# Six of layer 1's eleven pairs of up projections by Strassen's seven products, in three passes

## Chip, core and metric

One core of a Trainium2 chip runs the whole program. The metric is the device time of one execution in microseconds (us). The engines are TensorE (PE; its weight loads are listed apart as PEld), VectorE (DVE), ScalarE (ACT), GpSimd (POOL) and the DMA queue of SyncE (SP).

## What is computed

A trunk of two layers on 512 tokens of width 1024: layer 0 is a convolution module and a SwiGLU feed-forward part, layer 1 is windowed attention and a second SwiGLU part, then a last norm. The change is in the SwiGLU part of layer 1 alone:

```python
def swiglu_ffn(x, w_up, w_down):
    gate, up = jnp.split(x @ w_up, 2, axis=-1)
    return (jax.nn.silu(gate) * up) @ w_down

h = h + swiglu_ffn(rmsnorm(h, norm_ffn[l]), ffn_w_up[l], ffn_w_down[l])
```

`w_up` is 1024 x 5632 (gate and up, 2816 columns each), `w_down` is 2816 x 1024. All values are float32.

## The kernel before

**Layout.** Activations are kept transposed: a tile has 128 channels as partitions and the 512 tokens as columns. `h[0..7]` are the eight tiles of the residual. The norm's gain is applied to `h` before the projection (`split_scaled`, L431 and L432) and the factor 1/rms of each token after it.

**Three passes.** A float32 product is made from numbers cut into a high and a low part. `mm3` (L273 to L279) issues three matmuls for each 128x128 block of weights: high weights by high rows (L277), high weights by low rows (L278), low weights by high rows (L279), each with its own weight load. Here 512 columns of rows stream through each.

**Chunks.** Weights come as chunks of 128x1024 floats in the order of `PLAN`. `load` (L200) issues a chunk's DMA on SP into one of four `raw` buffers. `advance` cuts a chunk: ACT casts the high part (`whi`, L216), DVE subtracts it from the raw chunk (`wlo`, L219). It runs three chunks ahead of the one in use; `whi` and `wlo` have four buffers each, so a chunk is cut when PE is done with the chunk four places before it.

**Up projections.** The 2816 columns are eleven pairs of 128-column tiles. A pair has four chunks: contraction half 0 and 1, each for gate and for up (in the code `half` and `which`), and 96 matmuls. `ffn_up` ends a pair with the evacuation: DVE multiplies the four banks by 1/rms (L558, L560), ACT applies silu (L559), POOL multiplies gate by up (L561), and ACT and DVE cut the result into the hidden tile (L435, L436).

**Down projections.** After some pairs a part's down chunks follow (48 matmuls for each pair), and DVE adds the banks to `h` (L519). Before, layer 1 has the parts of pairs 0 to 5, 6 to 8, and the last two pairs 9 and 10, whose down projection is the block-wise end of the program (L1203, L1213).

**Around the first pair.** The output projection of attention ends in `h`. For each tile of `h`, `on_h` makes the cut and scaled rows (ACT L431, DVE L432) and a square (ACT L384) that is added up on POOL (L388). The sum over channels is a matmul (L398), then `ms` (DVE L400), the power -1/2 on POOL (L402), a diagonal (DVE L405), a matmul that spreads it (L424), and the copy `rsbc` (L418), which the evacuations need.

**Order.** The code gives the order in which work is issued; a scheduler at build time then orders the instructions of each engine by a timeline of its own, so an engine's queue can differ from the code. On the chip each queue runs strictly in order.

## Time and profile before

| | |
|---|---|
| three timed runs | median 1083.57 us (1082.81 to 1086.43) |
| the profiled execution | 1083.34 us, of which the span from first to last instruction is 1081.5 us |
| granted TensorE clock in it, mean | 0.999 of full speed |
| first sum over channels of layer 1's feed-forward part (L398) | at 722.20 us |
| start of its pair 1 (the spread of 1/rms stands just ahead) | 734.50 us |
| start of the block-wise end | 1050.43 us |
| HBM read, written | 118.20 MB, 5.24 MB |

A row of a group or of a timeline names the line of the kernel, the engine, the operation and the tiles (out <- in). In a group the mean of one is in ns; a timeline begins with the start and the length in us. Ends of matmuls are modelled, so PE's pace is read from the starts.

### The profile page before, as it was taken

The numbers are of one execution on the slowest core, as the hardware profiler recorded it, in microseconds if no ns is written. First come the engines' busy times: TensorE is split into PE (matmuls) and PEld (weight loads), VectorE is DVE, ScalarE is ACT, GpSimd is POOL, SyncE is SP. The second block draws the span as 40 slices with busy tenths as digits, with TensorE's granted clock in tenths as the row PEclk, the third lists the DMA queues.
The fourth block names the chain that finished last, engine by engine and source line by source line (L and its number), as shares of the span: only waits on it lengthen the run. The fifth ranks groups of instructions, "written<-read, shape, count | busy, mean of one in ns | idle before, by whom it ended". The sixth has DMA issues, their size and how long they took to land.

```text
span 1081.5 us, 14727 instructions
## 1 busy us (share of the span) xinstructions
PE 1074.3 (99%) x5506; PEld 913.0 (84%) x5506; DVE 633.6 (59%) x1034; ACT 490.0 (45%) x883; POOL 330.6 (31%) x430
## 2 busy tenths in 40 slices
PE   9999999999999999999999999999999999999997
PEld 8888889999988888888888777788888888888886
DVE  3999988977777545443555656564544333444353
ACT  3887887755565333232352655443323211322233
POOL 3999997710222111111120434141111100110010
PEclk9999999999999999999999999999999999999999
DMA  9238045565555422322222212222222222222202
GB/s 356 81 102 95 10 147 198 182 226 195 176 178 192 156 98 85 111 97 97 97 81 98 73 45 79 78 98 98 90 106 98 97 97 97 95 96 95 96 30 78
DMA packets 39555, 124.39 MB, mean 115 GB/s; under 512 B 4251, under 2 KB 10556, under 8 KB 39484
## 3 DMA queue, kind: packets, MB, share of 16 engines
q1 hardware_dynamic: 38764, 122.36, 33.7%
q10 hardware_dynamic: 720, 1.10, 0.3%
q8 instruction: 43, 0.70, 0.3%
q14 instruction: 28, 0.23, 0.1%
HBM read 118.20 MB, written 5.24 MB: 114 GB/s over the span
## 4 chain that ended last, share of the span: by engine, by line
PE 98%; issue 1%; DMA 1%; POOL 0%; ACT 0%; SPq 0%; POOLq 0%; DVE 0%
PE bank L277 23%; PE bank L278 23%; PE bank L279 23%; PE bank L674 10%; PE bank L309 5%; PE bank L275 4%; PE bank L310 3%; PE bank L1213 2%; PE bank L1071 1%; PE bank L1113 1%; PE bank L1100 1%; PE bank L772 1%; DMA both<-in_lead_dram 1%; PE bank L662 1%; PE bank L424 0%
## 5 line engine op out<-in xcount | busy, mean ns | idle before, releaser
L277 PE MATMUL bank<-quad,whi 128*128 128x512 f32 (+1 forms) x1200 | 439.2, 367 | 0.0
L279 PE MATMUL bank<-quad,wlo 128*128 128x512 f32 (+1 forms) x1200 | 439.0, 366 | 0.0
L278 PE MATMUL bank<-quad,whi 128*128 128x512 f32 (+1 forms) x1200 | 438.6, 365 | 0.0
L219 DVE TENSOR_TENSOR wlo<-raw,whi 128x1024 fp32r<-128x1024 f32 x186 | 258.0, 1388 | 303.2 <-ACT whi L216 298.7
L216 ACT CAST whi<-raw 128x1024 fp32r<-128x1024 f32 x186 | 195.3, 1050 | 358.2 <-PE bank L278 305.9
L277 PEld LDWEIGHTS bank<-quad,whi 128*128 128x128 f32 x1200 | 226.4, 189 | 37.7 <-issue 1.6
L279 PEld LDWEIGHTS bank<-quad,wlo 128*128 128x128 f32 x1200 | 226.4, 189 | 36.9 <-issue 0.6
L278 PEld LDWEIGHTS bank<-quad,whi 128*128 128x128 f32 x1200 | 226.4, 189 | 35.8 <-issue 0.2
L561 POOL TENSOR_TENSOR tmp<-tmp,tmp 128x512 f32<-128x512 f32 x34 | 48.1, 1416 | 408.8 <-DVE tmp L560 393.5
L716 POOL TENSOR_TENSOR pr<-pr,pr 128x256 f32<-128x256 f32 x208 | 156.5, 794 | 7.8 <-ACT pr L715 7.7
L723 DVE SCALAR_TENSOR_TENSOR bank<-apad,wdw,bank 128x256 f32<-128x256 f32 x248 | 112.6, 486 | 3.4
L715 ACT ACTIVATE pr<-apad,wdw 128x256 f32<-128x256 f32 x208 | 98.2, 501 | 14.7 <-POOL pr L716 12.7
L674 PE MATMUL bank<-quad,w 128*128 128x256 f32 x448 | 98.7, 380 | 0.0
L674 PEld LDWEIGHTS bank<-quad,w 128*128 128x128 f32 x448 | 84.9, 190 | 11.8 <-DVE bank L723 0.2
L388 POOL TENSOR_TENSOR tmp<-tmp,tmp 128x256 f32<-128x256 f32 (+1 forms) x35 | 38.6, 1103 | 149.1 <-ACT tmp L384 112.1
L309 PE MATMUL bank<-quad,whi 128*128 128x512 f32 x212 | 75.9, 398 | 0.0
L559 ACT ACTIVATE tmp<-tmp 128x512 f32<-128x512 f32 x34 | 21.4, 632 | 93.0 <-DVE tmp L558 93.0
L310 PE MATMUL bank<-quad,wlo 128*128 128x256 f32 x212 | 59.3, 280 | 0.0
L1090 POOL TENSOR_SCALAR sc<-sc,sm 128x256 f32<-128x256 f32 (+1 forms) x64 | 31.2, 507 | 52.9 <-DVE sm L1088 52.6
L309 PEld LDWEIGHTS bank<-quad,whi 128*128 128x128 f32 x212 | 39.7, 188 | 8.4
L560 DVE TENSOR_TENSOR tmp<-bank,rsbc 128x512 f32<-128x512 f32 x34 | 23.5, 691 | 32.4 <-PE bank L279 32.4
L310 PEld LDWEIGHTS bank<-quad,wlo 128*128 128x128 f32 x212 | 40.0, 189 | 1.3
(167 smaller groups left out, 921.2 us busy)
## 6 DMA issues: line engine op xcount, KB each, us to landing
raw<-in_W_dram SPq DMA_DIRECT2D x198, 512.0 KB, 3.5
w<-in_W_dram SPq DMA_DIRECT2D x14, 512.0 KB, 8.6
fd<-fs SPq DMA_DIRECT2D x1, 3072.0 KB, 34.0
h<-in_xT_dram SPq DMA_DIRECT2D x8, 256.0 KB, 8.6
bias<-fd SPq DMA_DIRECT2D x8, 256.0 KB, 4.5
both<-in_lead_dram SPq DMA_DIRECT2D x3, 512.0 KB, 6.3
out_dram<-hg SPq DMA_DIRECT2D x4, 256.0 KB, 2.0
out_dram<-hg ACTq DMA_DIRECT2D x4, 256.0 KB, 2.3
```

Of the source, the lines that this page charges most:

```text
L216: on_act = nc.scalar.copy(hi, r).ins
L219: latest[:] = [on_act, lo_engine[0].tensor_sub(lo, r, f32(hi)).ins]
L277: nc.tensor.matmul(out, w[0], x[0], start=start, stop=False)
L278: nc.tensor.matmul(out, w[0], x[1], start=False, stop=False)
L279: nc.tensor.matmul(out, w[1], x[0], start=False, stop=stop)
L309: nc.tensor.matmul(first[2], first[0], first[1], start=start, stop=False)
L310: nc.tensor.matmul(second[2], second[0], second[1], start=False, stop=stop)
L561: nc.gpsimd.tensor_mul(t2, t1, t2)
L674: mm = nc.tensor.matmul(self.pb[:, w * W2:(w + 1) * W2], w1_of(ct, w, k), x[k] if x else xg[k][:, tok], start=k == 0, stop=k == KT - 1)
L715: on_act = nc.scalar.mul(pr, a[:, j:j + W2], tap(j))
L716: on_pool = nc.gpsimd.tensor_add(pr, acc, pr)
L723: on_dve = nc.vector.scalar_tensor_tensor(yt if i == nd - 1 else c, src, tap(i), c if i else self.shift, op0=ALU.mult, op1=ALU.add)
```

## The change

Pairs 1, 3, 5, 6, 8 and 9 are made by Strassen's method in Winograd's form. The weights of a pair are a 2x2 block matrix: A11, A12, A21, A22, where the first index is the 128-column tile and the second the contraction half, each for gate and up side by side. The rows are B11 to B22, where the first index is the contraction half and the second the token half. Seven products take the place of eight. Each product is one chunk of 24 matmuls of 256 columns; a pair has 168. Pairs 0, 2, 4, 7 and 10 stay as before.

- Sums of weights, on POOL, each as two instructions of 128x512 (gate, up): S1 = A21 + A22, S2 = S1 - A11, S3 = A11 - A21, S4 = A12 - S2. They stand in the new pool `seven` (four buffers). A sum is cut by one cast and one subtraction as a chunk was; a plain block A11, A12 or A22 by two of each, of half the size.
- Sums of rows (`Rows.sums`): beside pair 0, ACT makes float32 copies of the eight scaled tiles (L724), POOL makes T1, T3, T2 and T4 from them (L731, 128x1024 each), and ACT and DVE cut each.
- Combination: each product is one bank. ACT copies the first and S1's product out, DVE adds the other five to the float32 tile `up` (L792 to L801, S2's product needs two), POOL adds twice (L794, L795). DVE multiplies by 1/rms in two instructions of 128x1024 (L805), then silu, product and cut as before.
- Raw chunks: the four chunks of such a pair stay in the four `raw` buffers till their last block is cut or summed.
- Parts: 0 to 2, 3 to 5, 6 to 8, then 9 and 10.
- The squares of the eight tiles are added up on DVE (L461) and not on POOL, and the sum over channels is issued after the first chunk of pair 0, not after the second.
- The DMA of the last norm's gain is the last load on SP, since its pool is now opened after pair 10.

```diff
-HALVES1 = ((0, 6), (6, 9))
+HALVES1 = ((0, 3), (3, 6), (6, 9))
+SEVEN = ("A11 B11", "S3 T3", "S1 T1", "S2 T2", "A12 B21", "S4 B22", "A22 T4")
+SEVENS = (1, 3, 5, 6, 8, 9)
+SEVEN_FIRST = ("A11 B11", "S1 T1", "S3 T3", "S2 T2", "A12 B21", "S4 B22", "A22 T4")
...
+            if name == "S1":
+                nc.gpsimd.tensor_add(s[name], a["A21"], a["A22"])
+            elif name == "S2":
+                nc.gpsimd.tensor_sub(s[name], s["S1"], a["A11"])
+            elif name == "S3":
+                nc.gpsimd.tensor_sub(s[name], a["A11"], a["A21"])
+            else:
+                nc.gpsimd.tensor_sub(s[name], a["A12"], s["S2"])
...
-        load(u + DMA_AHEAD)
-        while stream["split"] < min(len(PLAN), u + SPLIT_AHEAD):
+        load(SLOTS[min(len(SLOTS) - 1, u + SPLIT_AHEAD - 1)][0] + 1 + DMA_AHEAD - SPLIT_AHEAD)
+        while stream["split"] < min(len(SLOTS), u + SPLIT_AHEAD):
...
+            src = seven_sources(*blocks)
+            if len(src) == 1:
+                split_weights(hi, lo, src[0])
+                continue
+            for e in range(2):
+                split_weights(*(w[:, e * 512:(e + 1) * 512].rearrange("p (k c) -> p k c", k=4) for w in (hi, lo)), src[e])
...
+        def on_h(self, i):
+            split_scaled(self.x[i], h[i], col(self.gain, i))
+            self.rms.add(h[i])
+        def sums(self):
+            f = [quad(F32) for _ in range(2)]
+            for i in range(KT):
+                nc.scalar.mul(f[i // 4][:, i % 4, :], h[i], col(self.gain, i))
+            b11, b12, b21, b22 = (x[:, :, s] for x in f for s in HALF)
...
+            for name, t, f, a, b in (("T1", t1, nc.gpsimd.tensor_sub, b12, b11), ("T3", b12, nc.gpsimd.tensor_sub, b22, b12),
+                                     ("T2", b11, nc.gpsimd.tensor_add, b12, b11), ("T4", b21, nc.gpsimd.tensor_sub, b21, b11)):
+                f(t, a, b)
+                yield
+                both = quads.tile([P, 2, 4, 256], F32R, tag="quad", name=uid("rows"))
+                self.block[name] = [both[:, a] for a in range(2)]
+                split(self.block[name], t)
...
+            for n, name in enumerate(order_of(layer, pair)):
+                w = get_seven(layer, pair, n)
+                a, b = name.split()
+                x = rows.block[b]
+                r = acc[a] = bank().rearrange("p (a s) -> p a s", a=2)
+                for which in range(2):
+                    for k in range(4):
+                        mm3(r[:, which], [v[:, which, k, :] for v in w], [x[e][:, k, :] for e in range(2)],
+                            which == 0 and k == 0, which == 1 and k == 3)
+                if a == "A11":
+                    nc.scalar.copy(c11, r)
+                elif a == "S1":
+                    nc.scalar.copy(c22, r)
+                elif a == "S2":
+                    nc.vector.tensor_add(c12, r, c11)
+                    nc.vector.tensor_add(c21, acc["S3"], c12)
+                    nc.gpsimd.tensor_add(c12, c12, c22)
+                    nc.gpsimd.tensor_add(c22, c21, c22)
+                elif a == "A12":
+                    nc.vector.tensor_add(c11, r, c11)
+                elif a == "S4":
+                    nc.vector.tensor_add(c12, r, c12)
+                elif a == "A22":
+                    nc.vector.tensor_add(c21, r, c21)
...
+                nc.vector.tensor_mul(c[:, m], c[:, m], rs_bc)
+                gate = c[:, m, :, 0, :]
+                nc.scalar.activation(gate, gate, AF.Silu)
+                t = temp()
+                nc.gpsimd.tensor_mul(t.rearrange("p (s q) -> p s q", s=2), gate, c[:, m, :, 1, :])
+                split(hid[2 * (pair - lo) + m], t)
```

**What moves in the queues.** First PE, from the end of pair 0's first chunk to the start of its second, before the change. `quad1121` and `quad1122` are the high and low rows of contraction half 0, banks 1150 to 1153 the pair's four banks:

```order
L278 MATMUL bank1151_6658<-quad1122_6536,whi1135_6568 128x512
L279 MATMUL bank1151_6658<-quad1121_6535,wlo1136_6569 128x512
L277 MATMUL bank1152_6659<-quad1121_6535,whi1138_6598 128x512
L278 MATMUL bank1152_6659<-quad1122_6536,whi1138_6598 128x512
L279 MATMUL bank1152_6659<-quad1121_6535,wlo1139_6599 128x512
L277 MATMUL bank1153_6660<-quad1121_6535,whi1138_6598 128x512
```

The same place of PE with the change. `quad1112` and `quad1113` are the rows of contraction half 0, `quad1114` and `quad1115` those of half 1:

```order
L351 MATMUL bank1145_6655<-quad1113_6476,whi1135_6572 128x512
L352 MATMUL bank1145_6655<-quad1112_6475,wlo1136_6573 128x512
L350 MATMUL bank1144_6654<-quad1114_6477,whi1149_6660 128x512
L351 MATMUL bank1144_6654<-quad1115_6478,whi1149_6660 128x512
L352 MATMUL bank1144_6654<-quad1114_6477,wlo1150_6661 128x512
L350 MATMUL bank1144_6654<-quad1114_6477,whi1149_6660 128x512
```

Before, the second chunk still reads half 0; now it reads half 1, and the up part of half 0 (`whi1138`) comes third, behind the sum over channels.

POOL around pair 0, before: the last of the sums of squares, 1/rms, and the evacuations of pairs 0 and 1:

```order
L388 TENSOR_TENSOR tmp1142_6641<-tmp1141_6635,tmp1142_6641 128x512
L388 TENSOR_TENSOR tmp1143_6647<-tmp1142_6641,tmp1143_6647 128x512
L402 TENSOR_TENSOR rs1162_6728<-ms1161_6726,mhalf_141 128x4
L561 TENSOR_TENSOR tmp1172_6796<-tmp1171_6795,tmp1172_6796 128x512
L561 TENSOR_TENSOR tmp1174_6804<-tmp1173_6803,tmp1174_6804 128x512
```

With the change (L731 is T1, T3, T2, T4 in turn; L255, L259, L257, L261 are S1, S3, S2, S4):

```order
L731 TENSOR_TENSOR t11160_6739<-quad1158_6729 128x1024
L255 TENSOR_TENSOR sum1171_6789<-raw1137_6600,raw1155_6699 128x512
L259 TENSOR_TENSOR sum1183_6848<-raw1137_6600 128x512
L259 TENSOR_TENSOR sum1183_6848<-raw1148_6658 128x512
L257 TENSOR_TENSOR sum1187_6881<-sum1171_6789,raw1137_6600 128x512
L731 TENSOR_TENSOR quad1158_6729<-quad1159_6730,quad1158_6729 128x4x256
L255 TENSOR_TENSOR sum1171_6789<-raw1148_6658,raw1161_6741 128x512
L261 TENSOR_TENSOR sum1194_6945<-raw1155_6699,sum1187_6881 128x512
L475 TENSOR_TENSOR rs1153_6695<-ms1152_6693,mhalf_141 128x4
L731 TENSOR_TENSOR quad1158_6729<-quad1158_6729 128x4x256
L257 TENSOR_TENSOR sum1187_6881<-sum1171_6789,raw1148_6658 128x512
L731 TENSOR_TENSOR quad1159_6730<-quad1159_6730,quad1158_6729 128x4x256
```

Eight sums of weights and four of rows stand between the first of them and the evacuation of pair 0, and 1/rms (L475) stands among them.

POOL at the end of pair 5, before (the evacuations of pairs 4, 5 and 6, two instructions each):

```order
L561 TENSOR_TENSOR tmp1252_7356<-tmp1251_7355,tmp1252_7356 128x512
L561 TENSOR_TENSOR tmp1254_7364<-tmp1253_7363,tmp1254_7364 128x512
L561 TENSOR_TENSOR tmp1272_7496<-tmp1271_7495,tmp1272_7496 128x512
L561 TENSOR_TENSOR tmp1274_7504<-tmp1273_7503,tmp1274_7504 128x512
L561 TENSOR_TENSOR tmp1340_8016<-tmp1339_8015,tmp1340_8016 128x512
L561 TENSOR_TENSOR tmp1342_8024<-tmp1341_8023,tmp1342_8024 128x512
```

With the change (`raw1351` and `raw1354` are the first two chunks of pair 6; L809 is pair 5's product of gate and up):

```order
L795 TENSOR_TENSOR up1314_7827<-up1314_7827 128x512
L809 TENSOR_TENSOR tmp1342_8060<-up1314_7827 128x512
L259 TENSOR_TENSOR sum1372_8242<-raw1351_8104 128x512
L809 TENSOR_TENSOR tmp1343_8066<-up1314_7827 128x512
L259 TENSOR_TENSOR sum1372_8242<-raw1354_8134 128x512
```

A sum of pair 6 (L259, S3) now stands ahead of the second half of pair 5's evacuation. The same is found at the end of pair 8 with pair 9's S3.

More of the change, by code (lines that the diff above doesn't have):

```diff
@@ L49, with by_seven, order_of, ups @@
 NPARAM = _c
+SEVEN = ("A11 B11", "S3 T3", "S1 T1", "S2 T2", "A12 B21", "S4 B22", "A22 T4")
+SEVENS = (1, 3, 5, 6, 8, 9)
+SEVEN_FIRST = ("A11 B11", "S1 T1", "S3 T3", "S2 T2", "A12 B21", "S4 B22", "A22 T4")
+def by_seven(layer, pair):
+    return layer == 1 and pair in SEVENS
+def order_of(layer, pair):
+    return SEVEN_FIRST if pair == SEVENS[0] else SEVEN
+def ups(layer, pair):
+    return [("up", layer, pair, half, which) for half in range(2) for which in range(2)]
+def slot_plan(plan):
+    slots = []
+    for i, c in enumerate(plan):
+        if c[0] != "up" or not by_seven(c[1], c[2]):
+            slots.append((i, None))
+        elif c[3:] == (0, 0):
+            slots += [(i + (3 if n else 1), (c[1], c[2], n)) for n in range(7)]
+    return slots
 def chunk_plan():
@@ L61, in ffn @@
         for pair in range(lo, hi):
-            for half in range(2):
-                for which in range(2):
-                    plan.append(("up", layer, pair, half, which))
+            plan.extend(ups(layer, pair))
         for g in range(2):
@@ L82, in chunk_plan @@
                 plan.append(("o", part * 2 + kp, g))
-    ffn(1, *HALVES1[0])
-    ffn(1, *HALVES1[1])
+    for part in HALVES1:
+        ffn(1, *part)
     for pair in range(*LAST):
-        for half in range(2):
-            for which in range(2):
-                plan.append(("up", 1, pair, half, which))
+        plan.extend(ups(1, pair))
     for kp in range(*LAST):
@@ L95 @@
 PLAN = chunk_plan()
+SLOTS = slot_plan(PLAN)
+AT = {c: i for i, c in enumerate(PLAN)}
 NATIVE = {i for i in range(PLAN.index(("up", 0, 1, 0, 0)))}
@@ L477, in ffn_part @@
         lo, hi = (HALVES0, HALVES1)[layer][part]
-        hid = ffn_up(layer, lo, hi, xg, tok, rms, twin, plain)
+        hid = ffn_up7(layer, lo, hi, xg, pool7) if layer else ffn_up(layer, lo, hi, xg, tok, rms, twin, plain)
         w = tok.stop - tok.start
@@ new lines, in plain_pair @@
+    def plain_pair(layer, pair, rows, hid, i):
+        banks = accs(512)
+        steps = None
+        for half in range(2):
+            for which in range(2):
+                w = get("up", layer, pair, half, which)
+                order = [(k, m) for k in range(4) for m in range(2)]
+                if half == 1:
+                    order = [(k, m) for m in range(2) for k in range(4)]
+                for k, m in order:
+                    mm3(banks[which * 2 + m], [a[:, k, m * P:(m + 1) * P] for a in w], rows.x[half * 4 + k],
+                        half == 0 and k == 0, half == 1 and k == 3)
+                if half == 0 and which == 0:
+                    rows.rms.step1()
+                    continue
+                if pair == 0:
+                    steps = steps or rows.sums()
+                    for _ in range(1 + half):
+                        next(steps, None)
+        rs_bc = rows.rms.step2()
+        hid.grow()
+        for m in range(2):
+            t1, t2 = temp(), temp()
+            nc.vector.tensor_mul(t1, banks[m], rs_bc)
+            nc.scalar.activation(t1, t1, AF.Silu)
+            nc.vector.tensor_mul(t2, banks[2 + m], rs_bc)
+            nc.gpsimd.tensor_mul(t2, t1, t2)
+            split(hid[i + m], t2)
@@ new lines, in ffn_up7 @@
+    def ffn_up7(layer, lo, hi, rows, pool):
+        hid = Hidden()
+        rms = rows.rms
+        for pair in range(lo, hi):
+            if not by_seven(layer, pair):
+                plain_pair(layer, pair, rows, hid, 2 * (pair - lo))
+                continue
+            c = pool.tile([P, 2, 2, 2, 256], F32, tag="up", name=uid("up"), bufs=2)
+            c11, c12, c21, c22 = (c[:, m, s] for m in range(2) for s in range(2))
+            acc = {}
+            for n, name in enumerate(order_of(layer, pair)):
[3 more added lines that the diff above has]
+                r = acc[a] = bank().rearrange("p (a s) -> p a s", a=2)
+                for which in range(2):
+                    for k in range(4):
[16 more added lines that the diff above has]
+                    nc.vector.tensor_add(c21, r, c21)
+            rs_bc = rms.step2().rearrange("p (s q) -> p s q", s=2).unsqueeze(2).to_broadcast([P, 2, 2, 256])
+            hid.grow()
+            for m in range(2):
+                nc.vector.tensor_mul(c[:, m], c[:, m], rs_bc)
[4 more added lines that the diff above has]
+                split(hid[2 * (pair - lo) + m], t)
+        return hid
@@ L1149, in hybrid_trunk @@
             query(gp, jp, step)
-        nxt = Next(("ffn1",))
         for part in range(2):
@@ L1181, in hybrid_trunk @@
                 drain(pipe)
-    attn.close()
-    ffn_part(1, 0, nxt.x["ffn1"], ALL, nxt.rms)
-    ffn_part(1, 1, nxt.x["ffn1"], ALL, nxt.rms)
+                attn.close()
+                seven = ExitStack()
+                pool7 = sums_pool[0] = seven.enter_context(tc.tile_pool(name="seven", bufs=2))
+                nxt = Rows("ffn1", pool7)
+    for part in range(len(HALVES1)):
+        ffn_part(1, part, nxt, ALL, None)
+    hid = ffn_up7(1, *LAST, nxt, pool7)
+    seven.close()
     res = ctx.enter_context(tc.tile_pool(name="res", bufs=2))
```

54 lines of the change are left out of this document (45 added, 9 removed).

## The prediction

> **What bounds the kernel now.** I read the head of the page first, then its chain of waits.
>
> ```profile
> span 1081.5 us, 14727 instructions
> PE 1074.3 (99%) x5506; PEld 913.0 (84%) x5506; DVE 633.6 (59%) x1034; ACT 490.0 (45%) x883; POOL 330.6 (31%) x430
> ...
> PE 98%; issue 1%; DMA 1%; POOL 0%; ACT 0%; SPq 0%; POOLq 0%; DVE 0%
> ```
>
> PE is the bound: 98% of the chain. So a change pays if it takes time off PE and gives PE nothing to wait for. Next the busy time in three stretches: two with matmuls of 256 columns (layer 0, with DVE at 5.43 of 5.50 us, and the V projection), and layer 1's feed-forward part from pair 1 to the block-wise end.
>
> ```profile
> core 0: us, PE busy (x) PEld busy (x) DVE busy (x) ACT busy (x) POOL busy (x), PEclk, DMA share, GB/s
> 206.50:212.00 5.50, 5.50 (x48) 5.50 (x47) 5.43 (x9) 1.57 (x2) 3.13 (x4) 1.00 0.59 201
> 569.82:575.22 5.40, 5.40 (x48) 5.40 (x46) 4.12 (x7) 0.00 (x0) 1.93 (x1) 1.00 0.42 145
> 734.50:1050.43 315.93, 315.93 (x1394) 261.37 (x1393) 131.66 (x137) 87.92 (x103) 29.64 (x21) 1.00 0.26 92
> ```
>
> The last row holds, by the code, the up projections of pairs 1 to 10 (10 x 96) and the down projections of pairs 0 to 8 (9 x 48), 1392 matmuls of 512 columns; the count of 1394 takes in what runs over the edges. 315.93 / 1392 = 0.2270 us each, without a gap worth the name. There DVE is 42% busy, ACT 28%, POOL 9%: they have room. For the pace at 256 columns, the timeline of PE:
>
> ```profile
> 569.82 0.28 PE L277 MATMUL bank<-whi,quad 128*128 128x256 f32 x1
> ...
> 575.22 0.28 PE L277 MATMUL bank<-whi,quad 128*128 128x256 f32 x1
> ...
> 722.20 0.95 PE L398 MATMUL bank<-ones_c,tmp 128*128 128x1 f32 x8
> ```
>
> 45 steps in 5.40 us: 0.1200 us each, every one with its own weight load. The first window agrees (5.50 us for about 46, weights as the stationary side, DVE full beside it). Half the columns cost 53% of the time, not 50%.
>
> **The gain on PE.** A plain pair is 96 x 0.2270 = 21.79 us. A pair by seven products is 168 x 0.1200 = 20.16 us. Six pairs: 6 x 1.63 = 9.8 us. The down projections keep their number of matmuls; the further part adds eight additions to `h` on DVE (0.69 each, as L558 below), which run beside PE's next chunk and cost nothing: they delay only a cut that has 5 us to spare. The Trainium skill (TensorE: Matmul & The Clock Gate, Back-to-back issue gap) gives N/2.4 + 2.5 ns for an isolated warm matmul; by that estimate the pairs are 20.7 and 18.3 us and the six give 14 us, but both paces above disagree with it (227 and 120 ns against 216 and 109), and the rows decide.
>
> **What the other engines do for it.** Durations of the operations by line (minimum, median, maximum in ns), and two groups:
>
> ```profile
> L219 DVE TENSOR_TENSOR wlo<-raw,whi x186: 1193/1226/2325, 168.3 to 1051.8; 128x1024 fp32r<-128x1024 f32 x186
> ...
> L561 POOL TENSOR_TENSOR tmp<-tmp,tmp x34: 1285/1296/1598, 381.9 to 1051.8; 128x512 f32<-128x512 f32 x34
> ...
> L558 DVE TENSOR_TENSOR tmp<-bank,rsbc x34: 680/684/692, 375.6 to 1048.5; 128x512 f32<-128x512 f32 x34
> ...
> L436 DVE TENSOR_TENSOR quad<-tmp,quad x42: 418/679/1122, 235.8 to 1054.1; 128x512 fp32r<-128x512 f32 x34, 128x256 fp32r<-128x256 f32 x8
> ```
>
> ```profile
> L216 ACT CAST whi<-raw 128x1024 fp32r<-128x1024 f32 x186 | 195.3, 1050 | 358.2 <-PE bank L278 305.9 <-issue 22.0 <-PE bank L309 11.5
> L435 ACT CAST quad<-tmp 128x512 fp32r<-128x512 f32 x34 | 21.1, 621 | 26.6 <-POOL tmp L561 26.6
> ```
>
> Per pair by seven products, in 20.16 us:
> - DVE from SBUF alone: four subtractions of 128x1024 (4 x 1.23), six of 128x512 (6 x 0.68), two products with 1/rms (2 x 1.23), two of the hidden tiles (2 x 0.68): 12.8 us. From PSUM: five additions of 0.69: 3.4 us. Together 16.2.
> - POOL: eight sums, two combinations, two products, 12 x 1.30 = 15.6 us. (A plain pair has two, 2.6.)
> - ACT: 4 x 1.05 and twelve of about 0.62: 11.6 us.
>
> All fit, but DVE and POOL are not independent. The timeline shows it, POOL and DVE around the squares:
>
> ```profile
> 700.88 5.66 POOL L388 TENSOR_TENSOR tmp<-tmp,tmp 128x512 f32<-128x512 f32 x3 [21.82 <-ACT tmp L384]
> ...
> 703.06 2.32 DVE L219 TENSOR_TENSOR wlo<-raw,whi 128x1024 fp32r<-128x1024 f32 x1
> ...
> 707.01 1.21 DVE L219 TENSOR_TENSOR wlo<-raw,whi 128x1024 fp32r<-128x1024 f32 x1
> ...
> 709.61 0.76 DVE L432 SCALAR_TENSOR_TENSOR quad<-h,prm,quad 128x512 fp32r<-128x512 f32 x1
> ...
> 714.26 3.48 DVE L432 SCALAR_TENSOR_TENSOR quad<-h,prm,quad 128x512 fp32r<-128x512 f32 x2
> ```
>
> Beside POOL, a DVE instruction with both inputs in SBUF takes 2.32 us and not 1.21 (L432 1.74 and not 0.76), and POOL's take 1.89 and not 1.30. L558, with one input in PSUM, never exceeds 692 ns. The Trainium skill (SBUF — State Buffer, SBUF: two separate sides) calls the pair of ports an exclusive lock in just this case, held for a whole instruction; 1.21 + 1.30 = 2.5 us would be the worst wait by it, and 2.32 is near.
>
> **In the steady state I price this at nothing.** The queues put the sums early: a pair's raw chunks land (rows below) while the plain pair or the down chunks ahead of it run, so POOL makes the sums there, where a chunk lasts 5.4 us and DVE has one subtraction for it. Inside such a pair, DVE needs about 16.2 of 20.16 us, and chunks are cut up to three places ahead (3 x 2.88 = 8.6 us). If that cover is gone, the second rival tells the price.
>
> ```profile
> raw<-in_W_dram SPq DMA_DIRECT2D x198, 512.0 KB, 3.5
> w<-in_W_dram SPq DMA_DIRECT2D x14, 512.0 KB, 8.6
> ```
>
> On SP, the next chunks queue behind the buffers that such a pair holds. Those of half 0 are free when S2 is made. Those of half 1 are free when A22 is cut, which can begin as PE ends the third product; four products (11.5 us) are then left, less about 2.5 for the cut, and two further chunks of 5.4 us stand ahead of the one that lands there. A landing of 3.5 us fits, one of 8.6 as well. The gain's DMA now stands behind every weight chunk, waits for pair 9 and delays nothing behind it; its reader comes some 15 us later.
>
> **Where I expect a stall: pairs 0 and 1.** The order of PE puts the half-1 chunk second. Pair 0 starts at 722.20 - 48 x 0.227 = 711.3; row tile 7 of half 1, low part, was needed at about 723 and is now needed 24 + 20 matmuls after the start, at 721.3. Meanwhile it comes later. Before:
>
> ```profile
> 712.25 0.72 ACT L431 ACTIVATE quad<-h,prm 128x512 fp32r<-128x512 f32 x1
> 712.87 0.62 ACT L384 ACTIVATE tmp<-h 128x512 f32<-128x512 f32 x1
> 713.39 0.71 ACT L431 ACTIVATE quad<-h,prm 128x512 fp32r<-128x512 f32 x1
> ...
> 723.42 1.97 POOL L402 TENSOR_TENSOR rs<-ms,mhalf 128x4 f32<-128x4 f32 x1 [6.23 <-DVE ms L400]
> ```
>
> ACT makes the high part of tile 7 at 713.39; seven of the float32 copies for the sums of rows (L724, 0.62 each as L384 is) now stand ahead: 717.7, done at 718.4. Six of them also stand ahead of a chunk's cast, which began at 711.3 and now ends at 711.3 + 3.7 + 1.05 = 716.1. DVE then has that chunk's subtraction, tile 6, an addition, tile 7. Alone: 716.1 + 1.23 + 0.76 + 0.68 + 0.76 = 719.5, no stall. But T1 starts on POOL when four copies are made (about 713.8) and eleven sums follow in a row, so all of it may be contended: 716.1 + 2.32 + 1.74 + 1.3 (0.68 x 1.9) + 1.74 = 723.2, a stall of 1.9 us, and 0.4 more at the sum over channels (L471), which waits for one further addition. That these additions moved from POOL to DVE (seven of 0.68) is in this sum; it took POOL's 1.89 each out of the way of the tiles of half 0, which had time. Bounds 0 and 2.3. I take 2.0, since POOL's queue there is full.
>
> In pair 1, the chunk S2 T2 is fourth, due at 711.3 + 21.8 + 0.9 (sums and spread) + 2.0 + 8.6 = 744.6. On DVE its subtraction stands behind the cut of T4, the eleventh of POOL's row: alone 713.8 + 21.5 (four sums of rows of 2 x 1.30, since they are twice as wide, seven sums of weights of 1.30, 1/rms 1.97) = 735.3, then 1.05 + 2 x 1.23: 738.8, no stall. All contended (POOL's 19.5 x 1.46, DVE 2.32): 744.3 + 1.05 + 4.6 = 749.9, a stall of 5.3. DVE is not on SBUF all the while, so POOL's pace is nearer to alone; behind it the four evacuations of pair 0 (4 x 0.69) hold the next cut a little. I take 1.0.
>
> **Sum**, against the profiled execution's 1083.34 us (span 1081.5 and 1.8 around it; 0.2 below the median of 1083.57): 1083.34 - 9.8 + 2.0 + 1.0 = 1076.5 us.
>
> **Rivals.**
> 1. No stall at all (cover holds in pairs 0 and 1): 1083.34 - 9.8 = 1073.5. For: the sums of durations alone, above. Against: POOL's full queue. 0.19.
> 2. Slower: DVE and POOL take turns in every pair by seven products. If POOL is busy throughout, DVE needs 12.8 x 1.9 + 3.4 = 27.7 us for 20.16 of PE. It decides once a pair loses over 1.63 us; with no cover six pairs lose 7.5 each: 1083.34 - 9.8 + 45 = 1119; with a third of it, 1089. For: 12.8 + 15.6 us of turns exceed 20.16. Against: POOL's sums lie ahead of the pair. By the lock of the skill's page this would be 12.8 + 15.6 + 3.4 = 31.8 us, the same case. 0.07.
> 3. No change: the tails of pairs 5 and 8. POOL's second product of gate and up stands behind S3 of the next pair, which waits for a raw chunk. That buffer is free about 0.3 us after the pair's end; a landing of 3.5, then 1.9 + 1.9 + 0.6 + up to 2.3 + 1.1 is 11.6 us, and PE needs the tile after two down chunks, 10.9 us. With a landing of 8.6 it is 5.8 us late. The chain's own terms are contended ends, and at 3.5 us it is 0.7 late at most. Halfway, 3.2 us, twice: 1076.5 + 6.5 = 1083.0. Against: the median landing is 3.5, and the buffer's DMA runs alone. 0.11, some of it (0.03) below 1080.3.
> 4. The gain is not there: 256 columns at 21.79 / 168 = 0.130 us with these operands gives 1083. No row shows that pace. 0.03.
>
> **Numbers.** The forecast's case has the remaining 0.60. A measurement of this kernel can tell about 0.3% (3.2 us) from no change, so faster is below 1080.3: 0.60 + 0.19 + 0.03 = 0.82; same 0.08 + 0.03 = 0.11; slower 0.07. The range takes in rival 1 less 0.3 us, and above, the contended ends of both stalls (7.6 us: 1081.1): 1073.2 to 1081.1. Outside lie rival 2, half of 3 and most of 4.
>
> **What would show it.** Steps of 0.120 us in the six pairs, each about 20.2 us long; plain pairs at 21.8. A hole of PE in pair 0's second chunk, ending with a low-row matmul (L351) released by DVE (L505), of about 2 us; one of about 1 us in pair 1 released by the cut (L237). POOL idle for most of pairs 3, 5, 6, 8, 9. No wait of PE at the down chunks after pairs 5 and 8. I am wrong if the pace at 256 columns is not 0.120, or if holes stand in every such pair.

## The result, and the profile after

| | before | after |
|---|---|---|
| median of four runs each, on one chip | 1084.14 us (1082.81 to 1086.43) | 1075.45 us (1075.09 to 1076.35) |
| ratio of the runs | 1 | 0.9919, 95% interval 0.9900 to 0.9938 |
| the profiled execution | 1083.34 us, span 1081.5 | 1075.16 us, span 1073.4 |

The change makes the kernel 0.8% faster; the forecast was 1076.5 us. The head of the page after, and its chain of waits:

```profile
span 1073.4 us, 15809 instructions
PE 1064.6 (99%) x5938; PEld 925.8 (86%) x5938; DVE 722.7 (67%) x1107; ACT 523.6 (49%) x943; POOL 434.7 (40%) x487
...
PE 96%; issue 1%; ACT 1%; DVE 1%; DMA 1%; SPq 0%; POOLq 0%; POOL 0%; DVEq 0%
```

PE is still the bound, with 9.7 us less of work (1064.6 against 1074.3). The chain has given 2% to others, and the timeline shows at which place. For a common mark I take the last row of attention's products with the values; 96 matmuls of the output projection later, 22.2 us in both kernels, pair 0 starts. Of before, then of after:

```profile
689.11 1.52 PE L1113 MATMUL bank<-prt,vq 128*64 128x256 f32 x12
```

```profile
688.34 1.52 PE L1299 MATMUL bank<-prt,vq 128*64 128x256 f32 x12
```

So pair 0 starts at 711.31 and at 710.54, and from there to the end of the span it is 370.2 us before and 362.9 after. I use this length below, because what lies ahead of it is the same code in every kernel and still differs from execution to execution. The busy time by stage, of after (columns as in the prediction's table of stretches): from pair 1 to the block-wise end, then pairs 1, 3 and 4.

```profile
735.78:1042.25 306.47, 306.47 (x1826) 274.30 (x1825) 209.61 (x201) 114.30 (x151) 125.50 (x76) 1.00 0.29 100
735.78:756.36 20.58, 20.58 (x170) 20.34 (x169) 20.51 (x20) 12.48 (x18) 11.20 (x6) 1.00 0.21 72
810.79:830.94 20.15, 20.15 (x169) 20.15 (x168) 13.49 (x15) 8.90 (x12) 5.07 (x3) 1.00 0.28 99
830.94:852.73 21.79, 21.79 (x99) 18.03 (x97) 18.61 (x13) 7.69 (x12) 18.26 (x11) 1.00 0.29 103
```

The first row stands against 315.93 us of before: 9.46 less. Pairs 3, 5, 6, 8 and 9 take 20.15 us each, the plain pair 4 takes 21.79. POOL's sums lie in the plain pair (18.26 us busy) and not in the pair that uses them (5.07). Behind pair 0's start only two rows of PE carry a wait:

```profile
720.07 0.62 PE L350 MATMUL bank<-quad,whi 128*128 128x512 f32 x2
721.69 0.50 PE L351 MATMUL bank<-quad,whi 128*128 128x512 f32 x1 [1.00 <-DVE quad L505]
...
723.38 1.05 PE L471 MATMUL bank<-ones_c,tmp 128*128 128x1 f32 x8 [0.49 <-DVE tmp L461]
```

Pair 0 takes 735.78 - 710.54 = 25.24 us with the spread, 23.19 before (734.50 - 711.31): 2.05 us given back. The books between the spans: 0.8 less ahead of pair 0, 2.05 more in it, 9.46 less from pair 1 on, 0.1 more at the end, together 8.1 us less.

Pair 1 takes 0.43 us more than pair 3, but that is no wait. It lies in the step from its first matmul to its second, beside the end of the spread, and before has the same there:

```profile
734.50 0.79 PE L277 MATMUL bank<-quad,whi 128*128 128x512 f32 x1
735.13 0.40 PE L278 MATMUL bank<-quad,whi 128*128 128x512 f32 x1
```

```profile
735.78 0.69 PE L350 MATMUL bank<-quad,whi 128*128 128x256 f32 x1
736.31 0.28 PE L351 MATMUL bank<-quad,whi 128*128 128x256 f32 x1
```

The step takes 0.63 us before, where one of 512 columns takes 0.227, and 0.53 after, where one of 256 takes 0.120: 0.40 and 0.41 us more.

### The profile page after: what moved, and what is told of

It reads as the page before. It is cut to its first block, busy times and chain, and to the rows that moved or that the text cites. A ratio compares the mean times of both kernels' runs of the same rounds, so it can differ in the third digit from the quotient of the medians.

```text
span 1073.4 us, 15809 instructions
## 1 busy us (share of the span) xinstructions
PE 1064.6 (99%) x5938; PEld 925.8 (86%) x5938; DVE 722.7 (67%) x1107; ACT 523.6 (49%) x943; POOL 434.7 (40%) x487
## 4 chain that ended last, share of the span: by engine, by line
PE 96%; issue 1%; ACT 1%; DVE 1%; DMA 1%; SPq 0%; POOLq 0%; POOL 0%; DVEq 0%
PE bank L350 22%; PE bank L352 22%; PE bank L351 22%; PE bank L860 10%; PE bank L382 5%; PE bank L348 4%; PE bank L383 3%; PE bank L1403 2%; PE bank L1257 1%; PE bank L1299 1%; PE bank L1286 1%; PE bank L958 1%; PE bank L848 1%; DMA both<-in_lead_dram 1%; ACT quad L724 0%
## 5 line engine op out<-in xcount | busy, mean ns | idle before, releaser
L237 DVE TENSOR_TENSOR wlo<-raw,whi 128x1024 fp32r<-128x1024 f32 (+1 forms) x198 | 265.3, 1348 | 185.3 <-ACT whi L234 185.0
L351 PE MATMUL bank<-quad,whi 128*128 128x512 f32 (+1 forms) x1008 | 349.2, 346 | 1.0 <-DVE quad L505 1.0
L352 PE MATMUL bank<-quad,wlo 128*128 128x512 f32 (+1 forms) x1008 | 349.5, 347 | 0.0
L350 PE MATMUL bank<-quad,whi 128*128 128x512 f32 (+1 forms) x1008 | 349.4, 348 | 0.0
L234 ACT CAST whi<-raw 128x1024 fp32r<-128x1024 f32 (+1 forms) x198 | 190.3, 970 | 267.3 <-PE bank L351 209.4
L351 PEld LDWEIGHTS bank<-quad,whi 128*128 128x128 f32 x1008 | 191.1, 190 | 24.5 <-DVE quad L505 1.4
L350 PEld LDWEIGHTS bank<-quad,whi 128*128 128x128 f32 x1008 | 191.1, 190 | 24.5 <-issue 1.3
L352 PEld LDWEIGHTS bank<-quad,wlo 128*128 128x128 f32 x1008 | 191.0, 190 | 23.6 <-issue 0.6
L461 POOL TENSOR_TENSOR tmp<-tmp,tmp 128x256 f32<-128x256 f32 (+1 forms) x28 | 26.7, 955 | 123.1 <-ACT tmp L457 86.4
L237 DVE TENSOR_TENSOR wlo<-sum,whi 128x1024 fp32r<-128x1024 f32 x24 | 34.9, 1456 | 37.2 <-ACT whi L234 37.2
L351 PE MATMUL bank<-hid,whi 128*128 128x512 f32 x144 | 56.1, 390 | 0.0
L352 PE MATMUL bank<-hid,wlo 128*128 128x512 f32 x144 | 56.1, 389 | 0.0
L350 PE MATMUL bank<-hid,whi 128*128 128x512 f32 x144 | 55.8, 390 | 0.0
L352 PE MATMUL bank<-rows,wlo 128*128 128x256 f32 x192 | 54.4, 284 | 0.0
```

The lines of the kernel that those rows point to most:

```text
L234: on_act = nc.scalar.copy(hi, src).ins
L237: latest[:] = [on_act, lo_engine[0].tensor_sub(lo, src, f32(hi)).ins]
L350: nc.tensor.matmul(out, w[0], x[0], start=start, stop=False)
L351: nc.tensor.matmul(out, w[0], x[1], start=False, stop=False)
L352: nc.tensor.matmul(out, w[1], x[0], start=False, stop=stop)
```

## The experiments

Times are medians, ratios are against the kernel before on the same chip (its medians there lie between 1083.47 and 1084.14 us). The last column is the length from pair 0's start to the end of the span in the profiled execution.

| run | median us | ratio, 95% interval | from pair 0, us |
|---|---|---|---|
| before | 1084.14 | 1 | 370.2 |
| after | 1075.45 | 0.9919 (0.9900 to 0.9938) | 362.9 |
| after, again | 1076.15 | 0.9934 (0.9921 to 0.9946) | 362.9 |
| no_seven | 1083.87 | 0.9994 (0.9984 to 1.0004) | 370.3 |
| step_only | 1084.86 | 1.0007 (0.9998 to 1.0016) | 371.3 |
| copies_late | 1074.75 | 0.9914 (0.9900 to 0.9927) | 361.9 |
| mended | 1078.20 | 0.9948 (0.9935 to 0.9960) | 364.7 |
| power_first | 1076.50 | 0.9941 (0.9928 to 0.9955) | 363.6 |
| power_second | 1075.32 | 0.9922 (0.9909 to 0.9935) | 362.1 |
| sums_twice | 1077.95 | 0.9949 (0.9936 to 0.9961) | 363.1 |
| sums_twice_again | 1075.74 | 0.9928 (0.9914 to 0.9941) | 362.9 |
| nine | 1093.58 | 1.0092 (1.0078 to 1.0106) | 381.3 |
| nine_ready | 1093.22 | 1.0090 (1.0077 to 1.0103) | 380.6 |
| spaced | 1078.60 | 0.9957 (0.9945 to 0.9969) | 365.8 |

### no_seven: everything but the products

```diff
 def by_seven(layer, pair):
-    return layer == 1 and pair in SEVENS
+    return False
```

> All eleven pairs stay plain; the three parts, the squares on VectorE, the float32 copies and the row sums T1 to T4 beside pair 0 stay (the row sums are then read by nobody). Theory (the gain is the fewer matmul columns: six pairs by 1.63 us each, and what stands beside pair 0 only costs, about 1.8 us): 1083.3 + 1.8 = 1085 us, 1084 to 1086.5. Rival (part of the gain comes from the evacuation and the finer parts around the pairs, not from the products): 1080 us or less. In the profile every pair takes 21.8 us from chunk to chunk, and the hole in pair 0's second chunk is still there.

Measured: 1083.87 us, no difference from before. The gain comes from the products; the finer parts and the moved additions bring nothing that shows. But the hole in pair 0's second chunk is gone too, which the theory had not expected. DVE around tiles 6 and 7, of the changed kernel:

```profile
715.10 1.42 DVE L237 TENSOR_TENSOR wlo<-raw,whi 128x1024 fp32r<-128x1024 f32 x1 [2.46 <-ACT whi L234]
716.45 1.78 DVE L505 SCALAR_TENSOR_TENSOR quad<-h,prm,quad 128x512 fp32r<-128x512 f32 x1
718.15 1.79 DVE L461 TENSOR_TENSOR tmp<-tmp,tmp 128x512 f32<-128x512 f32 x1
719.87 1.77 DVE L505 SCALAR_TENSOR_TENSOR quad<-h,prm,quad 128x512 fp32r<-128x512 f32 x1
```

and without the products:

```profile
716.30 1.43 DVE L237 TENSOR_TENSOR wlo<-raw,whi 128x1024 fp32r<-128x1024 f32 x1 [2.46 <-ACT whi L234]
717.65 0.74 DVE L505 SCALAR_TENSOR_TENSOR quad<-h,prm,quad 128x512 fp32r<-128x512 f32 x1
718.31 0.68 DVE L461 TENSOR_TENSOR tmp<-tmp,tmp 128x512 f32<-128x512 f32 x1
718.92 0.74 DVE L505 SCALAR_TENSOR_TENSOR quad<-h,prm,quad 128x512 fp32r<-128x512 f32 x1
```

The float32 copies stand ahead on ACT in both, and DVE waits the same 2.46 us for the cast behind them. What differs is what POOL does at that time: with the products it goes from T1 straight into the sums of weights for pair 1, without them it is idle there. The three instructions to tile 7 then take 0.74, 0.68 and 0.74 us instead of 1.78, 1.79 and 1.77: 3.2 us. Counted from pair 0's start, tile 7's low part is ready after 11.1 us in the changed kernel (721.64 - 710.54) and after 7.9 here (719.66 - 711.73); PE asks for it after 44 matmuls, 10.0 us.

### copies_late: the float32 copies behind the last square

```diff
             for i in range(KT):
-                nc.scalar.mul(f[i // 4][:, i % 4, :], h[i], col(self.gain, i))
+                with tc.issue_after(self.rms.last):
+                    nc.scalar.mul(f[i // 4][:, i % 4, :], h[i], col(self.gain, i))
```

> The seven float32 copies of the normalized rows on ScalarE are held until the last square is issued; nothing else is changed. Theory (the copies ahead of tile 7 on ScalarE make its low part late, and so the hole in pair 0's second chunk): the hole of 1.2 us and the wait of 0.5 us behind the last sum of squares go; the row sums come some 3 us later, so that 1/rms and the cut of T4 become nearly late: 1073.6 to 1075.5 us. Rival (the hole is there because VectorE and GpSimd slow each other): the squares are still 1.8 us each, the hole stays at over 0.8 us, and the time is 1075 to 1076 us.

Measured: 1074.75 us, 361.9 from pair 0. Both waits of pair 0 are gone, with the sums of weights kept, and one is left:

```profile
733.58 1.12 PE L497 MATMUL bank<-tmp,ones_m 128*128 128x512 f32 x2 [0.86 <-DVE tmp L478]
```

As the theory had it, 1/rms is now what comes last. But this edit takes away two things. T1 is made from the copies, so POOL now starts behind tile 7, and DVE's row is as short as in no_seven. DVE, then POOL:

```profile
714.25 0.74 DVE L505 SCALAR_TENSOR_TENSOR quad<-h,prm,quad 128x512 fp32r<-128x512 f32 x1
```

```profile
715.73 2.41 POOL L732 TENSOR_TENSOR t<-quad 128x1024 f32<-128x1024 f32 x1 [38.13 <-ACT quad L725]
```

Tile 7's low part is ready at 714.99, 5.2 us after pair 0's start (709.83). No run takes away the copies alone. An estimate from these rows: with the 3.2 us that POOL added in the changed kernel it would be ready after 8.4 us, still ahead of the 10.0. So the hole needs POOL busy beside tile 7, which no_seven shows, and by this estimate also the copies ahead of it.

### step_only: the sum over channels one chunk later

```diff
                 if half == 0 and which == 0:
-                    rows.rms.step1()
                     continue
-
+                if half == 0:
+                    rows.rms.step1()
                 if pair == 0:
```

> Only the place of the last sum-of-squares matmuls is changed: they and what follows them are issued after the fourth chunk of pair 0 in program order instead of the third, which puts the half-1 chunk third on TensorE, as in the kernel before. Theory (the hole of 1.2 us in pair 0's second chunk is there because TensorE takes the half-1 chunk second, before tile 7's low part is made): that hole goes (-1.2 to -1.8 us), but 1/rms now stands behind two more row sums on GpSimd, and the spread of 1/rms at pair 0's end waits 2 to 4 us for it: 1075 to 1078 us in all. Rival (the hole comes from the slower VectorE and GpSimd rows alone, whatever the order of the chunks): the hole stays and moves to another chunk, and the time is 1077 us or more with a wait inside the chunks, not at the spread.

Measured: 1084.86 us; the whole gain is gone. The hole in the second chunk is gone as the theory said: tile 7's low part is ready after 11.1 us as in the changed kernel, and PE does not wait for it, so PE needs the tile later, as it would with the half-1 chunk third. The new wait stands at the spread, as it said too, but is of 8.33 us, not 2 to 4. On PE, POOL and DVE:

```profile
742.34 2.07 PE L497 MATMUL bank<-tmp,ones_m 128*128 128x512 f32 x2 [8.33 <-DVE tmp L478]
```

```profile
732.87 2.24 POOL L257 TENSOR_TENSOR sum<-sum,raw 128x512 f32<-128x512 f32 x1
735.08 2.00 POOL L475 TENSOR_TENSOR rs<-ms,mhalf 128x4 f32<-128x4 f32 x1
```

```profile
730.58 3.41 DVE L509 TENSOR_TENSOR rows<-quad,rows 128x1024 fp32r<-128x1024 f32 x1
733.92 0.15 DVE L473 TENSOR_SCALAR ms<-bank 128x4 f32<-128x4 f32 x1
733.99 3.34 DVE L237 TENSOR_TENSOR wlo<-sum,whi 128x1024 fp32r<-128x1024 f32 x2
737.25 3.35 DVE L509 TENSOR_TENSOR rows<-quad,rows 128x1024 fp32r<-128x1024 f32 x1
740.53 1.75 DVE L478 TENSOR_TENSOR tmp<-ident,rs 128x512 f32<-128x512 f32 x1
```

1/rms passes DVE, POOL, DVE, and I had counted only POOL's queue. The tiny `ms` (0.15 us) stands behind the cut of T3; the power behind a half of S2; the diagonal, whose power is done at 737.08, behind the cuts of sums of weights and of T2, 3.35 us for the last beside POOL. Three short steps in two full queues wait for a slot in each.

### mended: pair 0's evacuation behind the first product of pair 1

```diff
+        def finish():
+            rs_bc = rows.rms.step2()
...
+        if pair == 0:
+            return finish
+        finish()
...
                             which == 0 and k == 0, which == 1 and k == 3)
+                if rest:
+                    rest()
+                    rest = None
```

> The float32 copies are held behind the last square as in the run before, and pair 0's evacuation, with the spread of 1/rms, is issued after the first product of pair 1 instead of ahead of it. Theory (what is left at pair 1's start in the run before is the spread's wait for the diagonal, 0.86 us): that wait goes, 1073.3 to 1074.5 us. Rival (TensorE then waits for one of the four banks that pair 0 holds longer, or for the cut of T4, whose work stands in the same queues): 1075 us or more, with a wait inside pair 1.

Measured: 1078.20 us, 364.7 from pair 0; the rival. The wait at the spread is gone, and a longer one stands in pair 1, at the low weights of its sixth product, S4 B22. PE, then DVE:

```profile
752.30 0.39 PE L352 MATMUL bank<-quad,wlo 128*128 128x256 f32 x1 [2.20 <-DVE wlo L237]
```

```profile
748.01 2.02 DVE L509 TENSOR_TENSOR rows<-quad,rows 128x1024 fp32r<-128x1024 f32 x1
749.95 2.29 DVE L237 TENSOR_TENSOR wlo<-sum,whi 128x1024 fp32r<-128x1024 f32 x1
```

The four rows of the evacuation now stand later in DVE's queue (745.62 to 748.1, against 740.25 on in copies_late), and behind them the cuts of T4 and of S4 (the row at 749.95), for which PE waits.

### power_first and power_second: 1/rms earlier on POOL

Both keep the late copies. The first holds T3 behind the power, the second the two instructions of S2:

```diff
-                f(t, a, b)
+                with tc.issue_after(self.rms.pow) if name == "T3" else nullcontext():
+                    f(t, a, b)
```

```diff
-                nc.gpsimd.tensor_sub(s[name], s["S1"], a["A11"])
+                with tc.issue_after(power[0]):
+                    nc.gpsimd.tensor_sub(s[name], s["S1"], a["A11"])
```

> The float32 copies held behind the last square, as in the run with the late copies, and T3 held behind the power of 1/rms on GpSimd, so that the power stands one place earlier there and the diagonal three places earlier on VectorE. Theory (the 0.86 us wait at the spread in the run with the late copies comes from the power's place in GpSimd's queue): that wait goes and nothing else comes late: 1.0 to 2.0 us below the changed kernel, about 1074 us. Rival (T3 or the cut of S2 T2 is now late): a wait in pair 1 and no gain against the run with the late copies.

> The float32 copies held behind the last square, and the first half of S2 held behind the power of 1/rms on GpSimd, so that the power stands one place earlier there, behind T3, and the diagonal ahead of the cuts of T3 and S3 on VectorE. Theory (the wait at the spread goes, and unlike in the run before T3 is made at its old time, so that its cut has 5 us to spare): no wait of TensorE in pairs 0 and 1; 361 to 362 us from the start of pair 0 to the end of the span against 362.9 in the changed kernel and 361.9 in the run with the late copies; about 1074 us in all. Rival (VectorE, which waits at the diagonal with everything behind it, then makes the cut of T3 or of S2 late): a wait of 0.5 us or more in pair 1, 362.5 us or more.

Measured: 1076.50 and 1075.32 us, 363.6 and 362.1 from pair 0. In both the wait at the spread is gone. The first has two others in its place, at T2's low part in the fourth product and at the cut of S4 in the sixth:

```profile
744.89 0.38 PE L351 MATMUL bank<-rows,whi 128*128 128x256 f32 x1 [1.27 <-DVE rows L509]
752.05 0.39 PE L352 MATMUL bank<-quad,wlo 128*128 128x256 f32 x1 [0.58 <-DVE wlo L237]
```

and the second has one of 0.58 us, at the cut of S4 as well. The first is the rival. In the second the length (362.1) is nearer to the theory and the wait is the rival's, so it decides nothing between them. With the changed kernel these are six orders of the same work; they give 361.9 to 371.3 us, and none is without a wait. In the changed kernel DVE is busy for 20.51 of pair 1's 20.58 us (row above): what goes ahead there pushes something else behind.

### sums_twice: each sum of weights made twice

```diff
-                nc.gpsimd.tensor_add(s[name], a["A21"], a["A22"])
+                for _ in range(2 if pair > 1 else 1):
+                    nc.gpsimd.tensor_add(s[name], a["A21"], a["A22"])
```

and so for S2, S3 and S4.

> Each sum of weights of pairs 3, 5, 6, 8 and 9 is issued twice, which puts eight further instructions of 1.3 to 2.3 us on GpSimd for each pair. Theory (the sums lie beside the plain pair or the down chunks ahead, with room): less than 0.5 us more, 1075.4 to 1076 us. Rival (GpSimd and VectorE are near the point at which TensorE waits): 3 us or more, 1078 us and above.

The first median, 1077.95 us, lies 2.5 us above the changed kernel's, between the two theories. But the profile has no wait behind the two of pair 0, and the length from pair 0 is 363.1 us against 362.9. Nearly the whole difference of the profiled executions stands ahead of pair 0, so I ran it and the changed kernel again, side by side.

> The doubled sums once more, on the same chip as the changed kernel. Theory (they are hidden, and the 3.2 us ahead of pair 0 were of that one build or execution): within 0.5 us of the changed kernel from the start of pair 0 to the end of the span. Rival (they cost time in the pairs): 2 us or more from the start of pair 0.

> The changed kernel as it is, beside the two runs below. Theory (the 2.5 us by which the run with the doubled sums lay above it were time ahead of pair 0, which differs from execution to execution): 1075 to 1076.5 us; from the start of pair 0 to the end of the span 362.9 us within 0.3 unless the hole in pair 0 pulls the granted clock down. Rival (the level of the whole session was higher): 1077 us or more.

The mark ahead of pair 0 in the first and in the second execution of the doubled sums:

```profile
691.58 1.51 PE L1303 MATMUL bank<-prt,vq 128*64 128x256 f32 x12
```

```profile
688.79 1.52 PE L1303 MATMUL bank<-prt,vq 128*64 128x256 f32 x12
```

2.8 us apart with the same code; the medians then were 1075.74 and, for the changed kernel, 1076.15. So twice the sums cost nothing: behind a plain pair or down chunks there is room for them. And a difference of 2 us between two medians here can be time ahead of pair 0; the interval within one group of runs does not show that.

### nine: all pairs but the first and the last

```diff
-SEVENS = (1, 3, 5, 6, 8, 9)
+SEVENS = (1, 2, 3, 4, 5, 6, 7, 8, 9)
```

> Nine of layer 1's pairs go by seven products (all but the first and the last) instead of six. Theory (a pair by seven products leaves VectorE and GpSimd no room beside it for the next pair's sums, which lie in the plain pairs and the down parts now: 18.3 us of GpSimd in pair 4 against 5.1 us in pair 3): three more pairs take 4.9 us off TensorE, and waits of 2 to 5 us come at the starts of pairs that follow one by seven products directly, 1075 to 1085 us. Rival (the sums fit beside any pair, the slowing of VectorE and GpSimd by each other costs nothing): 1075.4 - 4.9 = 1070.5 us.

Measured: 1093.58 us, slower than before, and slower than the theory's 1085. Three such pairs in a row (3, 4 and 5), by busy time:

```profile
818.38:838.53 20.15, 20.15 (x169) 20.15 (x168) 13.30 (x15) 7.54 (x11) 6.02 (x4) 1.00 0.15 55
838.53:860.65 22.12, 20.68 (x171) 20.28 (x170) 17.68 (x17) 10.48 (x16) 16.87 (x11) 1.00 0.29 95
860.65:887.05 26.40, 22.60 (x170) 21.79 (x169) 20.57 (x21) 11.32 (x16) 20.69 (x11) 0.94 0.33 101
```

The one behind the down chunks loses nothing, the second 2.0 us, the third 6.2: each hands less of a lead to the next. Of the 6.2 us, 1.7 are not waits but the clock, which in 4 us of the third pair was granted at 0.53 and 0.62 (in stretches of 2 us: PE's busy time, then the clock):

```profile
874.00:876.00 2.00, 1.75 (x8) 0.53 0.41 160
876.00:878.00 2.00, 2.00 (x13) 0.62 0.00 0
```

POOL is at 6.02 us in the first pair and at 20.69 in the third. One reason could be that raw chunks come late, since such a pair holds all four buffers; POOL's first sum for pair 5 does wait for one:

```profile
859.15 1.30 POOL L255 TENSOR_TENSOR sum<-raw,raw 128x512 f32<-128x512 f32 x1 [5.25 <-DMA raw<-in_W_dram]
```

### nine_ready: the same, with sums that wait for no chunk

```diff
             s = {k: v[:, which] for k, v in sums.items()}
+            if pair > 1:
+                a = {k: stand[k[1]] for k in a}
```

> Nine pairs by seven products in a row as in the run with nine, but the sums of weights of pairs 2 to 9 are taken from one constant tile instead of the raw chunks (their values are then not the reference's; blocks that are cut directly still come from the chunks). The same instructions stand on GpSimd and VectorE. Theory A (the waits in the run with nine come from raw chunks that land late, since a pair holds all four buffers): most of the 23 us of waits go, 1071 to 1077 us. Theory B (they come from VectorE and GpSimd slowing each other): the waits stay, 1085 us or more.

The sums of weights of pairs 2 to 9 read one constant tile here, so this kernel leaves out the real sums; the instructions are the same. Measured: 1093.22 us; theory A falls. The waits move to other places, and the length from pair 0 is only 0.7 us less. DVE is now the bound. In the middle of the three pairs 3 to 5 it is busy for 22.27 of 22.30 us:

```profile
841.00:863.30 22.30, 22.30 (x189) 22.30 (x188) 22.27 (x19) 9.79 (x15) 18.50 (x11) 1.00 0.25 81
```

How far it is slowed is read over a whole part, three pairs by seven products and the down chunks ahead of them (786.70 to 885.65). Its groups of rows that belong to the pairs and have all inputs in SBUF:

```profile
L237 DVE TENSOR_TENSOR wlo<-sum,whi 128x1024 fp32r<-128x1024 f32 x12 | 21.5, 1794 | 10.0 <-ACT whi L234 10.0
L237 DVE TENSOR_TENSOR wlo<-raw,whi 128x512 fp32r<-128x512 f32 x18 | 21.4, 1220 | 2.6 <-ACT whi L234 2.6
L811 DVE TENSOR_TENSOR up<-up,rsbc 128x1024 f32<-128x1024 f32 x6 | 10.6, 1766 | 0.1
L515 DVE TENSOR_TENSOR hid<-tmp,hid 128x512 fp32r<-128x512 f32 x6 | 6.2, 1033 | 1.8 <-ACT hid L514 1.8
```

They take 59.7 us, 19.9 for each pair, where the prediction had 12.8 alone; with the five additions from PSUM (3.4) a pair needs 23.3 us of DVE.

The three pairs took 68.7 us with the real chunks and take 65.7 here. Of these 3.0 us, 1.7 are the clock of the run before (rows above); here it is granted in full through all the pairs. So 1.3 of the 8.2 us lost there are left for late chunks, and the clock's 1.7 only if it was their waits that brought it down, which no run separates. Pairs 1 and 2 lose 3.7 us more than in the run before (51.1 us against 47.3, by the starts of their first matmuls), perhaps since these sums start beside those of the rows; the 47.3 hold 1.7 us of lowered clock besides (0.58 and 0.57 in 768 to 772). What stays in either case is that DVE, slowed by POOL, has more than 20.16 us of work for a pair, and only a stretch in which it has little to do makes up for it.

### spaced: nine pairs, with one pair's down chunks between any two

```diff
+    plan.extend(ups(1, 0))
+    for pair in range(1, LAST[1]):
+        plan.extend(ups(1, pair))
+        if pair <= LAST[0]:
+            plan.extend(("down", 1, pair - 1, g) for g in range(2))
```

> Nine pairs by seven products (1 to 9), but each pair's down projection now stands behind the next pair's up projection, so that 10.9 us of down chunks (48 matmuls) lie between any two pairs by seven products. Theory (in the run with nine pairs in a row the waits come because nothing stands between two such pairs in which the next raw chunks can land and be summed): 1075.4 - 3 x 1.63 = 1070.6 us, 1070 to 1072.5, every pair at 20.2 us. Rival (the turns of VectorE and GpSimd are too many whatever lies between; 48 further additions to h on VectorE make it worse): waits of 1 to 3 us stay in each of eight pairs, 1078 to 1090 us.

Measured: 1078.60 us, 365.8 from pair 0: the rival's time, though not its waits of 1 to 3 us in each pair. The gap of 10.9 us takes most of the waits of nine away (eight pairs of 20.5 to 20.9 us, one of 22.73), but not all, and the additions to `h`, eight for each pair, fill DVE. A pair and the down chunks behind it, 31.47 us:

```profile
791.87:823.34 31.47, 31.32 (x219) 29.23 (x217) 28.08 (x30) 12.68 (x18) 21.25 (x12) 1.00 0.30 100
```

DVE is busy for 28.08 of 31.47 us, and a pair loses some 0.5 us of the 1.63 that it brings. The books against the changed kernel: 4.9 less for three more pairs; 6.1 more in the nine (187.9 us against 9 x 20.16, less the 0.4 of pair 1 that both have); 1.6 more in pair 0, where the clock fell (last section); 0.2 at the down chunks: 3.0 more. Six pairs, each behind a longer stretch, do better than nine. More raw buffers, the other remedy, were not tried.

## Why the prediction was right

- **Bound and pace: right.** Pairs of 20.15 and 21.79 us were forecast as 20.16 and 21.79. By an estimate from the Trainium skill's isolated gap (TensorE: Matmul & The Clock Gate, Back-to-back issue gap) a pair by seven products would take 18.3 us; the trace of after disagrees, with 20.15, as that of before did.
- **Gain 9.8 us: right.** Five pairs take 1.64 us less than a plain pair, and pair 1 takes 1.59 less than before (20.58 against 22.17, from 734.50 to 756.67). The whole stretch takes 9.46 less. The 0.3 between is the pace of the plain matmuls: a plain pair takes 21.79 us here and 21.76 before ((315.93 - 0.40) x 96 / 1392).
- **Steady state at nothing: right, for the reason given.** The sums lie ahead (18.26 us of POOL in pair 4), and doubling them is free. The reason carries further than I had put it: the cover is the stretch ahead, and with nine pairs it is gone.
- **Stall in pair 0, 2.0 us: right in place, releaser and total; the parts are sized otherwise.** It is 2.05 us, L351 released by L505 and then L471 by L461. PE was due at L351 after 44 steps, at 720.53, and began it at 721.69: 1.2 us where the working had 1.9. L471 came 0.7 us late where it had 0.4. In the chain to tile 7 the chunk's subtraction took 1.42 us, not 2.32, and the addition behind it 1.79, not 1.3. That the total is met within 0.1 us is luck in part. Of the causes that the step named, POOL busy beside tile 7 is shown (no_seven); the half-1 chunk in second place is shown (step_only fills the hole by moving it); the copies ahead of it on ACT rest on an estimate, since copies_late moves POOL's work too.
- **Stall in pair 1, 1.0 us: there is none.** This is the mis-sized term of the sum. No row of PE in pair 1 carries a wait, and its 0.43 us beside the spread stand in before as well (rows above). The cut of S2 T2 in the changed kernel:

```profile
742.89 1.21 DVE L237 TENSOR_TENSOR wlo<-sum,whi 128x1024 fp32r<-128x1024 f32 x1
```

It ended at 744.10, and PE came to the product at 735.78 + 3.27 + 2 x 2.88 = 744.81: 0.7 us to spare. It was near: with another order power_first waits 1.27 us at this product, for T2.
- **What is left of the difference:** 1.0 us of that term, and 0.8 us ahead of pair 0, which no step spoke of and which other executions have with either sign; against them 0.3 less gain and 0.1 at the end: 1076.5 - 1.0 - 0.8 + 0.3 + 0.1 = 1075.1, against 1075.16 of the profiled execution.
- **Rival 2 (DVE and POOL take turns) was false for this kernel and true one step further.** In nine the pairs lose 0, 2.0 and 6.2 us (1.7 of it the clock); I had put 7.5 on each. DVE needed 23.3 us for a pair (nine_ready), not 27.7: the 12.8 from SBUF alone grew to 19.9, by 1.55 and not by 1.9. POOL was not busy all the while there (61.26 of 98.95 us).
- **Rival 3 (tails of pairs 5 and 8) was false**: no row of PE at the down chunks carries a wait. **Rival 4 (the pace) was false.** Rival 1 (no stall) fails by pair 0.

Of the versions tried, the late copies are the best: 1.0 us less than the changed kernel from pair 0 in the profile. The medians, 1074.75 against 1075.45 and 1076.15, agree in sign, but their intervals overlap.

## What to carry to other kernels

Strassen's method for a bound TensorE moves work to engines that share something, and what decided here is not their busy share but whether a stretch with little for them lies ahead of each such block: six blocks with a gap beat nine in a row by 18 us, a lower clock behind the waits of the nine included. Where two engines' queues are both full, moving one step forward only moves the wait; take something away or spread it. A short step that goes back and forth between two full queues costs a slot in each, so count all of them before moving it.
